# The prologue's 56 stores, moved from SyncE's queue to GpSimd's

## The chip, the cores and the metric

The kernel runs on one core of a Trainium2 chip. Its time is the device time of one execution in microseconds (us), as a median over several runs. The core has five engines that matter here, each working through its own instruction stream in order: TensorE (PE in the profile) multiplies matrices and loads its weights (PEld), VectorE (DVE) and ScalarE (ACT) work element by element, GpSimd (POOL) does likewise but cannot reach the matmul accumulators, and SyncE (SP) computes nothing and only starts transfers. Data move between the chip's main memory and the on-chip memory by DMA transfers. A transfer is started by an instruction in some engine's stream; the data then move by themselves, and a semaphore tells when they have landed.

## The reference, cut to what matters

The reference is one layer of a decoder, run for a prompt of 2048 tokens and for a sample group of 8 sequences with 8 new tokens each, all in float32 with width 1024. The part that the change touches is the memory that the cross-attention reads:

```python
def _mem_kv(mem, g_mem, w_ck, w_cv):
    B = mem.shape[0]
    hm = _rmsnorm(mem, g_mem)
    k = (hm @ w_ck).reshape(B, N_MEM, N_CROSS_HEADS, CROSS_HEAD_DIM)
    v = (hm @ w_cv).reshape(B, N_MEM, N_CROSS_HEADS, CROSS_HEAD_DIM)
    return k, v
...
    x = x + jnp.concatenate([attn_o, pool_o], axis=-1) @ w_out
    h = _rmsnorm(x, g_cross)
    q = (h @ w_cq).reshape(B, L, N_CROSS_HEADS, CROSS_HEAD_DIM)
    s = jnp.einsum('blhd,bmhd->bhlm', q, mem_k).astype(jnp.float32) * (CROSS_HEAD_DIM ** -0.5)
    p = jax.nn.softmax(s, axis=-1)
    o = jnp.einsum('bhlm,bmhd->blhd', p.astype(mem_v.dtype), mem_v).reshape(B, L, D_MODEL)
    x = x + o @ w_co
```

The memory has 256 tokens. Its keys and values `mem_k` and `mem_v` are results of the function as well and must be written out. Beside this the layer has sliding-window attention with 8 heads, a pooling mixer over four windows, and a squared-ReLU MLP of width 4096; these make up most of the work, and the change does not touch them.

## The kernel before

**Number format.** Every product is made of three matmuls (helper `mm3`, lines 110 to 115, and the same pattern in `dense`, lines 317 to 319): each operand is split into a rounded high part and the rest, and high times high, high times low and low times high are added up in one accumulator.

**Weights.** All weights come through one stream (class `Stream`). `emit` (lines 127 to 137) takes one of six staging buffers `f`, starts a load of 512 KB on SyncE's queue (line 133), lets ScalarE round it (line 134) and VectorE take the difference (line 135), and gives the buffer back. Up to five split weights wait ready ahead of TensorE.

**The prologue** (lines 401 to 484) runs first. It has these stages:

1. keys and values of the memory: 16 products with `w_ck` and `w_cv`. `evac` (line 425) multiplies each by the norm on VectorE into a buffer `t` (line 427), stores it to `mk` or `mv` (line 429), and splits it for later use. These are 8 + 8 stores of 128 KB.
2. the fold of `w_cq` with the keys into a matrix A, kept in main memory as `a_s`: 8 weights, two products each, 16 stores of 256 KB.
3. the fold of the values with `w_co` into a matrix B, kept as `b_s`: 4 heads, two weights and four products each, 16 stores of 256 KB.

The fold of the pooling weights with the lower half of `w_out` (function `fold`, line 388) comes a little later, between the first products of the first superblock: four folds with two products each, 8 stores of 256 KB to `wo_s`.

All 40 fold stores go through `put_fold` (line 369): it takes a staging buffer `f` out of the same six that the weight loads use, ScalarE copies the accumulator into it (line 371), a store is started (line 373), and the buffer goes back to the end of the line. Whoever takes that buffer next has to wait until the store has landed. In stage 3 and in `fold` a store goes to four separate places, each row of 128 elements, 512 bytes:

```python
            put_fold(ps[:], lambda o: [(wo_s[4 * eh:4 * eh + 4, :, P * g:P * g + P].rearrange("e p c -> p e c"),
                                        o[:, 0:512].rearrange("p (e c) -> p e c", c=P))])
```

In stage 2 a row of a store is 512 elements, 2 KB, in one piece. The products themselves live in four accumulators `mm`, taken in rotation: a group of matmuls can start when the group four before it has been copied out.

**After the prologue** three superblocks follow, each with the combined input projection (line 879), window attention, the output projection with `woa` and `wo_s`, cross-attention with A and B read back from `a_s` and `b_s`, and the MLP. In them GpSimd scales attention rows (line 746) and adds up the pooling windows (lines 642 to 672).

**Order of the work.** The program order above is the priority, and a planner places the instructions of each engine in the order in which it takes them to become ready. All transfers of the kernel before are started on SyncE's queue, in one order; an instruction there that waits for its data holds up those behind it. The on-chip space for descriptors of transfers begun elsewhere is set where the program is made (line 1390):

```python
    nc = bacc.Bacc("TRN2", target_bir_lowering=False, num_devices=1, dynamic_dma_scratch_size=1024)
```

Of the kernel before, what the change touches and what calls it, by code (L numbers as in the profile page):

```python
# [51 lines left out]
def kernel(ctx: ExitStack, tc: tile.TileContext, io, nW=12, nF=6, nT=8):  # L52
    nc = tc.nc
# [39 lines left out]
    def f32(ap):  # L93
        return ap.bitcast(F32)

    def rnd(ps, hi, lo, scale=None):
        if scale is None:
            nc.scalar.copy(hi, ps)
            nc.vector.tensor_tensor(lo, ps, f32(hi), ALU.subtract)
        else:  # L100
            nc.scalar.activation(hi, ps, AF.Copy, scale=scale)
            nc.vector.scalar_tensor_tensor(lo, ps, scale, f32(hi), ALU.mult, ALU.subtract)
# [4 lines left out]
    def w8(t):  # L107
        return t[:].rearrange("p (k c) -> p k c", c=P)

    def mm3(ps, ks, Wh, Wl, Hh, Hl, first=True, final=True):  # L110
        last = len(ks) - 1
        for i, k in enumerate(ks):
            nc.tensor.matmul(ps, Wh(k), Hh(k), start=first and i == 0, stop=False)  # L113
            nc.tensor.matmul(ps, Wh(k), Hl(k), start=False, stop=False)  # L114
            nc.tensor.matmul(ps, Wl(k), Hh(k), start=False, stop=final and i == last)  # L115
# [226 lines left out]
    def flush(all_=False):  # L342
        for x in list(later):
            x[0] -= 1
            if all_ or x[0] <= 0:
                later.remove(x)
                g = x[1]()
                if g is None:
                    continue
                if all_:  # L350
                    run(g)
                elif next(g, 1) is None:
                    later.append([1, lambda g=g: g])
# [15 lines left out]
    def put_fold(ps, dsts):  # L369
        o = FS.get()  # L370
        nc.scalar.copy(o[:, 0:512], ps)
        for dst, src in dsts(o):
            nc.sync.dma_start(dst, src)
        FS.put(o)

    def prep_fold():
# [11 lines left out]
    def fold(g, wpr):  # L388
        th, tl = S.next(("wop", g))
        for eh in range(2):  # L390
            ps = MM.get()
            mm3(ps[:], [0], lambda k: wpr[:, P * g:P * g + P], lambda k: wpr[:, 512 + P * g:512 + P * g + P],
                lambda k: th[:, 512 * eh:512 * eh + 512], lambda k: tl[:, 512 * eh:512 * eh + 512])
            put_fold(ps[:], lambda o: [(wo_s[4 * eh:4 * eh + 4, :, P * g:P * g + P].rearrange("e p c -> p e c"),
                                        o[:, 0:512].rearrange("p (e c) -> p e c", c=P))])
            MM.put(ps)
        WS.put(th, tl)
        if g == 3:
            WS.put(wpr)

    def prologue():
        S.resW, S.resF = 1, 0
        mx = [XT[1][:, 0:1024], XT[1][:, 1024:2048]]
        mem = lambda k: mx[k // 4][:, 256 * (k % 4):256 * (k % 4 + 1)]
        warm = AUX.get()
        for _ in range(14):
            wu = nc.tensor.matmul(warm[:, 0:P], ones[:], ident[:], start=True, stop=True)
        AUX.put(warm)
        nc.sync.dma_start(vec[:], io["vec"])
        nc.sync.dma_start(mx[0][:, 0:512], io["mem"][:, 0:512])  # L410
        S.emit()
        hm = Act(256)
        nm = Norm(256, mem, add=nc.vector)
        for i in range(4):
            if i:
                nc.sync.dma_start(mx[i // 2][:, 512 * (i % 2):512 * (i % 2) + 512], io["mem"][:, 512 * i:512 * (i + 1)])
            for k in range(2 * i, 2 * i + 2):
                g = vec[:, V_GMEM + k:V_GMEM + k + 1]
                nc.scalar.activation(hm.hi(k), mem(k), AF.Copy, scale=g)
                nc.vector.scalar_tensor_tensor(hm.lo(k), mem(k), g, f32(hm.hi(k)), ALU.mult, ALU.subtract)  # L420
        S.emit()
        for k in range(8):
            nm.sq(k)
        S.pump()
        def evac(a, dst, c, ps):
            t = TS.get()
            nc.vector.tensor_tensor(t[:, 0:256], ps[:, 0:256], nm.r[:, 0:256], ALU.mult)
            MM.put(ps)
            nc.sync.dma_start(dst[:, 256 * c:256 * (c + 1)], t[:, 0:256])
            rnd(t[:, 0:256], a.hi(c), a.lo(c))  # L430
            TS.put(t)

        pend, outs = [], []
        for name, dst in (("ck", io["mk"]), ("cv", io["mv"])):
            a = Act(256)
            outs.append(a)
            for c in range(8):
                th, tl = S.next((name, c))
                ps = MM.get()
                with ExitStack() as held:  # L440
                    if (name, c) == ("ck", 0):
                        held.enter_context(tc.issue_after(wu.ins))
                    mm3(ps[:, 0:256], range(8), lambda k: w8(th)[:, k, :], lambda k: w8(tl)[:, k, :], hm.hi, hm.lo)
                WS.put(th, tl)
                pend.append((a, dst, c, ps))
                if name == "ck" and c == FINC:
                    nm.fin()
                if name == "cv" or c >= FINC:
                    while pend:
                        evac(*pend.pop(0))  # L450
                flush()
                if (name, c) == N1C:
                    norm1(blk[0][0], N1W)
        TS.put(nm.r)
        hm.free()
        mk, mv = outs
        norm1(blk[0][1], N1Q)
        for c in range(8):
            th, tl = S.next(("cq", c))
            for hf in range(2):  # L460
                ps = MM.get()
                for h2 in range(2):
                    ks = [(hf * 2 + h2) * 2, (hf * 2 + h2) * 2 + 1]
                    mm3(ps[:, 256 * h2:256 * h2 + 256], ks, lambda k: w8(th)[:, k, :], lambda k: w8(tl)[:, k, :], mk.hi, mk.lo)
                put_fold(ps[:], lambda o: [(a_s[hf, c // 2, :, 512 * (c % 2):512 * (c % 2) + 512], o[:, 0:512])])
                MM.put(ps)
            WS.put(th, tl)
            flush()
        mk.free()
        for h in range(4):  # L470
            w = [S.next(("co", 2 * h)), S.next(("co", 2 * h + 1))]
            for mb in range(2):
                for eh in range(2):
                    ps = MM.get()
                    mm3(ps[:], range(2),
                        lambda k: mv.hi(2 * h + k, mb * P, mb * P + P), lambda k: mv.lo(2 * h + k, mb * P, mb * P + P),
                        lambda k: w[k][0][:, 512 * eh:512 * eh + 512], lambda k: w[k][1][:, 512 * eh:512 * eh + 512])
                    kt = h * 2 + mb
                    put_fold(ps[:], lambda o: [(b_s[4 * eh:4 * eh + 4, :, P * kt:P * kt + P].rearrange("e p c -> p e c"),
                                                o[:, 0:512].rearrange("p (e c) -> p e c", c=P))])  # L480
                    MM.put(ps)
                flush()
            WS.put(*w[0], *w[1])
        mv.free()
# [17 lines left out]
    def norm1(bl, wait=2):  # L502
        n = bl.n
        if bl.s == 0:
            xs = []
            load_x(bl)
            nm = Norm(n, bl.x)
        else:
            xs = [FS.get() for _ in range(4)]
            for i in range(4):  # L510
                nc.sync.dma_start(xs[i][:, 0:2 * n], io["x"][:, bl.xo + 2 * i * n:bl.xo + 2 * (i + 1) * n])
            nm = Norm(n, lambda k: xs[k // 2][:, n * (k % 2):n * (k % 2) + n])
        for k in range(8):
            nm.sq(k)

        def rest():
            nm.fin()
            bl.h1 = Act(n)
            yield from nm.apply(V_GMIX, bl.h1.hi, bl.h1.lo, PIECE0 if bl.s == 0 else PIECE[0][bl.b])
            FS.put(*xs)  # L520

        later.append([wait, rest])
# [896 lines left out]
```

## Time and profile before

| | before |
|---|---|
| median of 3 runs | 2575.44 us (2572.5 to 2576.32) |
| the profiled execution's own time | 2575.38 us |
| span of its profile | 2573.6 us |
| TensorE busy | 2534.6 us, 98% |
| VectorE, ScalarE, GpSimd busy | 54%, 39%, 7% |
| granted TensorE clock | 0.996 of full |

The span runs from the first to the last instruction of the trace; the execution's own time is 1.8 us longer. "Busy" counts computing instructions only, and matmuls overlap in the pipeline, so that TensorE's 98% is the share of time in which some matmul was under way.

### The profile page before, as it was taken

The numbers are of one execution on the slowest core, as the hardware profiler recorded it, in microseconds if no ns is written. First come the engines' busy times: TensorE is split into PE (matmuls) and PEld (weight loads), VectorE is DVE, ScalarE is ACT, GpSimd is POOL, SyncE is SP. The second block draws the span as 40 slices with busy tenths as digits, with TensorE's granted clock in tenths as the row PEclk, the third lists the DMA queues.
The fourth block names the chain that finished last, engine by engine and source line by source line (L and its number), as shares of the span: only waits on it lengthen the run. The fifth ranks groups of instructions, "written<-read, shape, count | busy, mean of one in ns | idle before, by whom it ended". The sixth has DMA issues, their size and how long they took to land.

```text
span 2573.6 us, 36150 instructions
## 1 busy us (share of the span) xinstructions
PE 2534.6 (98%) x14241; PEld 2315.0 (90%) x14241; DVE 1388.7 (54%) x2797; ACT 998.9 (39%) x2013; POOL 167.4 (7%) x282
## 2 busy tenths in 40 slices
PE   9999999999999999999999999999999999999997
PEld 8798989999999999896788888899989888888886
DVE  8568545444434468774554546887445444434435
ACT  6666343322222234753442324475344322222222
POOL 0015010000000000411000000024010000000000
PEclk9999999999999999999999999999999999999999
DMA  8833212111111125146722222414111111111101
GB/s 284 266 121 102 91 37 78 66 66 66 58 65 66 50 66 160 50 168 213 283 98 93 97 99 75 155 32 148 42 62 54 66 58 58 63 60 58 58 25 54
DMA packets 97614, 245.09 MB, mean 95 GB/s; under 512 B 18916, under 2 KB 37796, under 8 KB 96420
## 3 DMA queue, kind: packets, MB, share of 16 engines
q1 hardware_dynamic: 97444, 242.78, 28.3%
q8 instruction: 112, 1.84, 0.3%
q14 instruction: 58, 0.48, 0.1%
HBM read 219.79 MB, written 22.95 MB: 94 GB/s over the span
## 4 chain that ended last, share of the span: by engine, by line
PE 56%; DVE 2%; ACT 1%; DMA 1%; POOL 0%; issue 0%; DVEq 0%; POOLq 0%; ACTq 0%
PE mm L318 10%; PE mm L317 10%; PE mm L319 10%; PE mm L114 7%; PE mm L113 7%; PE mm L115 7%; PE aux L724 1%; PE aux L755 1%; DVE x L1253 0%; PE aux L968 0%; PE aux L1052 0%; PE aux L114 0%; DVE w L135 0%; PE aux L113 0%; PE aux L115 0%; PE aux L1090 0%
## 5 line engine op out<-in xcount | busy, mean ns | idle before, releaser
L317 PE MATMUL mm<-act,w 128*128 128x384 f32 (+3 forms) x2528 | 857.1, 339 | 2.5 <-ACT act L679 1.6
L319 PE MATMUL mm<-act,w 128*128 128x384 f32 (+3 forms) x2528 | 851.4, 337 | 1.9 <-DVE w L135 1.9
L318 PE MATMUL mm<-act,w 128*128 128x384 f32 (+3 forms) x2400 | 801.8, 334 | 0.7 <-DVE act L680 0.7
L134 ACT CAST w<-f 128x1024 fp32r<-128x1024 f32 x330 | 346.5, 1051 | 818.2 <-PE mm L114 278.3
L113 PE MATMUL mm<-act,w 128*128 128x384 f32 (+3 forms) x1472 | 506.1, 344 | 3.2 <-ACT t L204 2.2
L115 PE MATMUL mm<-act,w 128*128 128x384 f32 (+3 forms) x1472 | 504.8, 343 | 1.9 <-DVE w L135 1.9
L317 PEld LDWEIGHTS mm<-act,w 128*128 128x128 f32 x2528 | 476.7, 189 | 28.3 <-ACT act L679 1.9
L319 PEld LDWEIGHTS mm<-act,w 128*128 128x128 f32 x2528 | 476.4, 188 | 23.1 <-DVE w L135 2.7
L135 DVE TENSOR_TENSOR w<-f,w 128x1024 fp32r<-128x1024 f32 x330 | 402.7, 1225 | 154.7 <-ACT w L134 76.9
L318 PEld LDWEIGHTS mm<-act,w 128*128 128x128 f32 x2400 | 452.6, 189 | 21.1 <-issue 2.5
L114 PE MATMUL mm<-act,w 128*128 128x384 f32 (+3 forms) x1344 | 454.1, 338 | 0.0
L1235 DVE TENSOR_TENSOR x<-mm,x 128x384 f32<-128x384 f32 (+2 forms) x448 | 199.2, 468 | 297.3 <-PE mm L115 297.2
L113 PEld LDWEIGHTS mm<-act,w 128*128 128x128 f32 x1472 | 277.1, 188 | 25.3 <-ACT t L204 2.4
L115 PEld LDWEIGHTS mm<-act,w 128*128 128x128 f32 x1472 | 277.1, 188 | 23.0 <-DVE w L135 2.3
L114 PEld LDWEIGHTS mm<-act,w 128*128 128x128 f32 x1344 | 253.0, 188 | 15.8
L1200 DVE SCALAR_TENSOR_TENSOR t<-mm,t 128x384 f32<-128x384 f32 (+3 forms) x224 | 99.8, 468 | 275.6 <-PE mm L319 275.5
L1201 ACT ACTIVATE t<-t 128x384 f32<-128x384 f32 (+3 forms) x224 | 95.1, 450 | 249.8 <-DVE t L1200 249.8
L1204 DVE TENSOR_TENSOR act<-t,act 128x384 fp32r<-128x384 f32 (+3 forms) x192 | 87.8, 477 | 88.9 <-ACT act L1203 88.9
L113 PE MATMUL mm<-w,act 128*128 128x512 f32 x288 | 114.8, 402 | 1.4 <-ACT w L134 1.3
L114 PE MATMUL mm<-w,act 128*128 128x512 f32 x288 | 113.1, 393 | 1.9 <-DVE w L135 1.8
L115 PE MATMUL mm<-w,act 128*128 128x512 f32 x288 | 112.8, 392 | 0.0
L266 ACT ACTIVATE act<-x,vec 128x384 fp32r<-128x384 f32 (+3 forms) x104 | 57.7, 563 | 106.5 <-DVE x L940 56.4
(210 smaller groups left out, 2200.5 us busy)
## 6 DMA issues: line engine op xcount, KB each, us to landing
f<-in_wup SPq DMA_DIRECT2D x96, 512.0 KB, 3.3
f<-in_wdn SPq DMA_DIRECT2D x96, 512.0 KB, 3.2
f<-in_win SPq DMA_DIRECT2D x30, 512.0 KB, 3.5
f<-a_s SPq DMA_DIRECT2D x24, 512.0 KB, 4.2
f<-b_s SPq DMA_DIRECT2D x24, 512.0 KB, 4.2
x<-in_x SPq DMA_DIRECT2D x6, 1536.0 KB, 8.1
f<-in_wco SPq DMA_DIRECT2D x16, 512.0 KB, 5.3
f<-in_cmk SPq DMA_DIRECT2D x16, 512.0 KB, 4.2
```

What stands on the lines that cost most here:

```text
L113: nc.tensor.matmul(ps, Wh(k), Hh(k), start=first and i == 0, stop=False)
L114: nc.tensor.matmul(ps, Wh(k), Hl(k), start=False, stop=False)
L115: nc.tensor.matmul(ps, Wl(k), Hh(k), start=False, stop=final and i == last)
L134: nc.scalar.copy(th[:], r[:, 0:1024])
L135: eng.tensor_tensor(tl[:], r[:, 0:1024], f32(th[:]), ALU.subtract)
L317: nc.tensor.matmul(ps[:, 0:n], w8(th)[:, k, :], hi(b, k), start=k == 0, stop=False)
L318: nc.tensor.matmul(ps[:, 0:n], w8(th)[:, k, :], lo(b, k), start=False, stop=False)
L319: nc.tensor.matmul(ps[:, 0:n], w8(tl)[:, k, :], hi(b, k), start=False, stop=k == 7)
L1200: nc.vector.scalar_tensor_tensor(r[:, 0:n], ps[:, o:o + n], 0.0, p.bl.r3[:, p.c0:p.c0 + n], ALU.max, ALU.mult)
L1201: nc.scalar.activation(q[:, 0:n], r[:, 0:n], AF.Square)
L1204: nc.vector.tensor_tensor(lo, q[:, 0:n], f32(hi), ALU.subtract)
L1235: nc.vector.tensor_tensor(p.x(m), ps[:, p.o:p.o + p.n], p.x(m), ALU.add)
```

## The change

Two lines start their transfers from GpSimd's queue (`nc.gpsimd`) instead of SyncE's (`nc.sync`). The first is in `put_fold`, which makes the 40 stores of fold products, the second in `evac`, which makes the 16 stores of memory keys and values. Sources, destinations, sizes and buffers stay as they are, and all loads stay on SyncE's queue.

```diff
@@ -370,7 +370,7 @@
         o = FS.get()
         nc.scalar.copy(o[:, 0:512], ps)
         for dst, src in dsts(o):
-            nc.sync.dma_start(dst, src)
+            nc.gpsimd.dma_start(dst, src)
         FS.put(o)
@@ -426,7 +426,7 @@
             t = TS.get()
             nc.vector.tensor_tensor(t[:, 0:256], ps[:, 0:256], nm.r[:, 0:256], ALU.mult)
             MM.put(ps)
-            nc.sync.dma_start(dst[:, 256 * c:256 * (c + 1)], t[:, 0:256])
+            nc.gpsimd.dma_start(dst[:, 256 * c:256 * (c + 1)], t[:, 0:256])
             rnd(t[:, 0:256], a.hi(c), a.lo(c))
             TS.put(t)
```

## The prediction

> **What bounds the kernel now.** I read the page's first lines, then the busy time by stretches of the prologue, then what TensorE waits for there, then the transfers.
>
> ```profile
> span 2573.6 us, 36150 instructions
> PE 2534.6 (98%) x14241; PEld 2315.0 (90%) x14241; DVE 1388.7 (54%) x2797; ACT 998.9 (39%) x2013; POOL 167.4 (7%) x282
> ...
> core 0: us, PE busy (x) PEld busy (x) DVE busy (x) ACT busy (x) POOL busy (x), PEclk, DMA share, GB/s
> 63.00:90.00 27.00, 25.53 (x190) 23.86 (x190) 22.34 (x36) 20.27 (x39) 0.46 (x1) 1.00 0.81 253
> 90.00:118.00 28.00, 25.44 (x110) 19.34 (x109) 10.09 (x11) 16.33 (x25) 0.00 (x0) 1.00 0.96 287
> 118.00:145.00 27.00, 24.00 (x118) 21.16 (x117) 15.15 (x22) 16.59 (x28) 0.00 (x0) 0.94 0.76 233
> ```
>
> TensorE sets the time, with 2534.6 of 2573.6 us. The change acts between 24 and 145 us. The three stretches are the A fold, the B fold, and the first input products with the pooling folds; in them TensorE lacks 1.5 + 2.6 + 3.0 = 7.1 us. That is the most a better order of transfers there can give. In the B stretch the DMA engines are at 96%: there the transfers themselves fill the time.
>
> ```profile
> PE mm L113 <- ACT t L204: 2.2, 1, 2.2
> PE mm L113 <- ACT w L383: 2.0, 1, 2.0
> PE mm L115 <- DVE w L135: 1.9, 2, 1.2
> PE mm L114 <- DVE w L135: 1.8, 3, 0.8
> ```
>
> Of TensorE's waits up to 165 us (total, times, longest) the first is a norm and has no transfer in it; the other three are for weights that came late.
>
> ```profile
> SPq L373 <- ACT f L371: 28.6, 25, 4.6
> SPq L429 <- DVE t L427: 28.2, 15, 6.2
> ```
>
> These are SyncE's own waits at the moved lines: 57 us in which the store at the head of the queue waited for ScalarE's or VectorE's copy, with loads queued behind it. That is what the change takes away.
>
> **The change part by part.** It moves 56 instructions that start transfers: 16 in `evac`, 40 in `put_fold`. No store becomes smaller, and no load moves.
>
> ```profile
> L373 SPq DMA_DIRECT2D a_s<-f x16: 319/326/1625, 65.0 to 87.7; - x16
> L373 SPq DMA_DIRECT2D b_s<-f x16: 359/498/1901, 90.5 to 116.3; - x16
> L373 SPq DMA_DIRECT2D wo_s<-f x8: 359/377/422, 125.9 to 141.4; - x8
> ```
>
> (Shortest, median and longest start in ns, first and last start.) On SyncE they take some 0.33 to 0.50 us each, about 20 us for the 40; SyncE is no bound, so this saving is worth nothing by itself. On POOL there is room:
>
> ```profile
> 54.61 0.25 POOL L612 COPY x<-ucar 128x15 f32<-128x15 f32 x1 [53.31 <-DVE t L258]
> ...
> 69.68 0.46 POOL L612 COPY x<-ucar 128x15 f32<-128x15 f32 x1 [7.49 <-DVE t L258]
> 163.36 1.11 POOL L746 TENSOR_SCALAR x<-x,st 128x128 f32<-128x128 f32 x3 [93.22 <-DVE st L742]
> ```
>
> POOL computes nothing in the prologue except four copies that are wanted only later; the first work that TensorE will wait for is L746 at 163.4 us. What a start costs on POOL, the trace does not show. Bounds: 0.32 us (the shortest start on SP) and 2.2 us (the shortest landing of these stores, below). The B stage brings 16 stores in 28 us, one per 1.75 us, so any price up to 1.75 us is hidden. I take about 1 us, nearest to the 4.16 us that four waiting starts took on SP (next fence), and count nothing for it.
>
> Removed waits: without the stores ahead of them the loads may start earlier. The bounds are a gain of 7.1 us, were all the lacking TensorE time to go, and nothing, since loads also wait for one of the six `f` buffers, and these wait for landings:
>
> ```profile
> 90.47 4.16 SPq L373 DMA_DIRECT2D b_s<-f  x4
> ...
> 69.12 1.21 ACT L371 COPY f<-mm 128x512 f32<-128x512 f32 x2 [2.08 <-DMA a_s<-f]
> ...
> 104.96 1.20 ACT L371 COPY f<-mm 128x512 f32<-128x512 f32 x2 [0.20 <-DMA b_s<-f]
> ```
>
> ScalarE already waits here for an `f` buffer whose store has not landed. So the term that decides is how long a store holds its buffer.
>
> ```profile
> q1 hardware_dynamic: 8894, 7.99, 95.2%
> ...
> b_s<-f SPq DMA_DIRECT2D x16, 256.0 KB, 5.6
> ...
> a_s<-f SPq DMA_DIRECT2D x16, 256.0 KB, 4.4
> ...
> wo_s<-f SPq DMA_DIRECT2D x8, 256.0 KB, 3.0
> ...
> out_mk<-t SPq DMA_DIRECT2D x8, 128.0 KB, 2.4
> ...
> DMA to landing us min/median/max: 2.2/4.8/6.2
> ```
>
> (The first two lines are of 90 to 118 us: packets, MB, share; then KB each and median us to landing.) In that stretch 16 stores and 7 loads make 8894 packets: a store of 256 KB in rows of 512 bytes is 512 packets, 8192 together, and the loads have the rest, some 100 each. The stores of `wo_s` have the same form, those of `a_s`, `mk` and `mv` are 128 rows each.
>
> On SP up to four such stores are under way at a time, one for each `f` buffer that is not with a load (in the B stage four stores and two loads share the six). On POOL the trace shows no transfer, so I bound from both sides: they overlap as on SP, or a store of 512 packets starts only when the one before it has landed. I take the second for `b_s` and `wo_s`, and overlap for the others: the code reserves 1024 bytes (line 1390) for describing such transfers, and 512 packets are much to describe in that, 128 four times less. [...]
>
> The price of one at a time: let T be the time from a store's start to the next one's. The 24 stores (16 B, 8 pooling) then land at 90.5 + kT. With four buffers, the copy of store 22 needs store 18 landed, and the first input product behind the last fold needs that copy, by the rotation of four `mm`. Before, that product started here:
>
> ```profile
> 140.54 0.33 PE L317 MATMUL mm<-act,w 128*128 128x384 f32 x1
> ```
>
> With 0.6 us for the copy (two took 1.21 us above), TensorE is late by 90.5 + 18T + 0.6 - 140.5 = 18T - 49.4 us. T lies between 3.0 us (`wo_s`, same form and size) and 5.6 us (`b_s` at 95% DMA load, with loads ahead of it in its own queue). One at a time the engines are less full, so I start from 3.0 us and add the start of about 1 us, which nothing overlaps: T = 4.0 us, and 18 x 4.0 - 49.4 = 22.6 us. The ends are 4.6 us (T = 3.0) and 51.4 us (T = 5.6). Nothing later gives it back, as TensorE is busy 98% of the span.
>
> What is late next:
>
> ```profile
> 149.97 0.43 SPq L133 DMA_DIRECT2D f<-wo_s  x1
> 167.44 0.33 SPq L133 DMA_DIRECT2D f<-in_woa  x1
> ```
>
> The first read of `wo_s` needs all folds landed: 90.5 + 24 x 4.0 = 186.5 us, against 150.0 + 22.6 = 172.6. SyncE stands 14 us there, but the next load behind it is not wanted before 167.4 + 22.6 = 190 us, so this is hidden up to T = 4.1 us, and beyond that five ready weights cover it. On POOL the last store starts at 90.5 + 23 x 4.0 = 182.5 us, ahead of L746 at 163.4 + 22.6 = 186: hidden, by 2.5 us net of the start.
>
> Sum: the profiled execution's 2575.38 us (0.06 below the median of the runs shown) + 22.6 = 2598.0 us.
>
> **The rivals.** *The stores overlap on POOL as on SP* and SyncE's loads start earlier: between 2575.4 - 7.1 = 2568.3 and 2575.4 us. The 57 us of waits speak for it. Against a large gain speak the 96% DMA share of the B stage, which leaves at most the 1.5 and 3.0 us of its neighbours, 2.0 of which hang on L383's one late load. I'd expect 2572. It decides as soon as two 512-packet stores can be under way. This is the rival on the other side.
>
> *One at a time, but quick.* Below T = 49.4 / 18 = 2.74 us TensorE is not held, and the time stays at 2575.4. The shortest landing of 2.2 us and `mk`'s 2.4 us speak for it; both `b_s` and `wo_s` medians lie above. [...]
>
> *A start on POOL costs over 1.75 us.* At the upper bound of 2.2 us the B stage takes 16 x 2.2 - 28 = 7.2 us more: 2582.6 us. The longest start on SP, 1.9 us, would cost 2.4 us.
>
> *All 40 fold stores go one at a time.* Then store 34 of the 40, counted from the first `a_s` at 65.0 us, is the one waited for: 65.0 + 34T + 0.6 - 140.5 = 34T - 74.9; with T = 3.0, for 128 rows are lighter, 27.1 us: 2602.5. The smaller packet count of `a_s` speaks against it.
>
> **How the numbers follow.** One at a time with T above 3.03 us: 0.57. Overlap: 0.20, half of it a gain of over 0.2%, half none. Quick: 0.10. POOL's start: 0.07. All 40: 0.06. About 0.2%, 5.2 us, is what a measurement of this kernel can tell from no change. Slower is 0.57 + 0.07 + 0.06 = 0.70, the same 0.10 + 0.10 = 0.20, faster 0.10. The range reaches from 2571, which takes in most of the overlap case, to 2627, T = 5.6; the forecast's own range is 2580 to 2627.
>
> **What would show it.** In the changed profile: L373 on POOL's queue; `b_s` starts 3 to 5.6 us apart instead of 1.75, each after the landing before it; `a_s` starts as close as before; ScalarE's L371 waiting for `b_s` landings by many us; the B stretch of TensorE stretched, its idle time there some 20 us; the rest of the trace shifted and otherwise the same. I am wrong if two `b_s` stores are under way at once, if the time lost lies after 190 us, or if the A stretch grows as much as the B stretch.

## The result

The changed kernel is **slower**, by 1.3%: 2608.41 us, median of 4 runs (2607.21 to 2612.48), against 2575.88 us for the kernel before beside it (4 runs, 2572.5 to 2576.88). The difference of the medians is 32.5 us; the ratio on record, which is not worked out from the two medians alone (they give 1.0126), is 1.0132, with a 95% interval of 1.012 to 1.0144. One of the ten executions of act_queue below took 3113 us and is left out of its figures; with it its median is 2578.74 us. The forecast was 2598.0 us, or 22.6 us slower, with a range of 2571 to 2627. The side and the mechanism were right, the size was 10 us short, and the forecast came that near partly by luck (see the part on the prediction).

The profiled execution took 2612.48 us, 4.1 us more than its kernel's median. Numbers read from the trace below are therefore a little larger than the 32.5 us that the medians show.

The first lines of the page after, and its DMA queues (packets, MB, share):

```profile
span 2610.7 us, 36174 instructions
...
PE 2546.5 (98%) x14241; PEld 2326.2 (89%) x14241; DVE 1388.3 (53%) x2797; ACT 999.5 (38%) x2013; POOL 202.1 (8%) x338
...
q1 hardware_dynamic: 80164, 230.19, 25.5%
q0 software_dynamic: 3968, 12.59, 1.4%
```

The move happened: POOL has 56 more instructions, and a queue of the software kind carries the 12.59 MB. TensorE's matmuls are the same in number; the span grew by 37.1 us, its busy time by 11.9 us, so two thirds of the loss is idle time of TensorE.

Busy time by stretches, after (columns as in the prediction; the last row is a new stretch):

```profile
63.00:90.00 27.00, 25.17 (x188) 24.41 (x187) 21.37 (x34) 18.72 (x35) 8.48 (x17) 0.94 0.73 239
90.00:118.00 28.00, 20.36 (x79) 13.75 (x77) 10.40 (x14) 13.97 (x22) 6.42 (x9) 1.00 0.59 203
118.00:145.00 27.00, 16.03 (x70) 13.27 (x69) 5.44 (x9) 8.60 (x16) 6.06 (x8) 0.87 0.38 122
145.00:165.00 20.00, 9.02 (x35) 8.27 (x35) 7.33 (x10) 7.34 (x12) 3.78 (x5) 0.66 0.52 163
```

The A fold, 63 to 90 us, is nearly as before (25.17 us busy against 25.53). Behind it TensorE lacks 28.00 - 20.36 = 7.6 us, then 11.0 and 11.0 us. The DMA share, 0.96 in the B stretch before, is 0.59: the transfers no longer fill the time, they wait to be started. In the last two rows the granted clock has fallen as well, to 0.87 and 0.66.

The moved instructions themselves (shortest, median, longest in ns, first and last start; then what POOL's idle time before them ended with, and who waited for them):

```profile
L373 POOL DMA_DIRECT2D a_s<-f x16: 542/542/552, 66.7 to 93.2; - x16
L373 POOL DMA_DIRECT2D b_s<-f x16: 752/761/784, 95.3 to 145.2; - x16
L373 POOL DMA_DIRECT2D wo_s<-f x8: 752/757/762, 150.3 to 179.9; - x8
...
  issue: 59.3, 21
...
  ACT f L371: 36.9, 16
```

The 16 `b_s` stores, which started within 25.8 us before, now take 49.9 us, or 49.87 / 15 = 3.32 us apart; the 8 of `wo_s` are 29.6 / 7 = 4.23 us apart. A start itself is short, 0.54 us with 128 rows and 0.76 us with 512. Yet POOL sat idle for 59.3 us in front of 21 of them for "issue", that is for nothing that the profile shows. POOL's timeline (start, duration, idle time before and its releaser):

```profile
66.74 2.42 POOL L373 DMA_DIRECT2D a_s<-f  x4 [3.08 <-ACT f L371]
...
95.33 0.78 POOL L373 DMA_DIRECT2D b_s<-f  x1 [1.62 <-ACT f L371]
...
110.03 0.76 POOL L373 DMA_DIRECT2D b_s<-f  x1 [2.32 <-issue]
113.05 0.75 POOL L373 DMA_DIRECT2D b_s<-f  x1 [2.26 <-issue]
...
179.90 0.75 POOL L373 DMA_DIRECT2D wo_s<-f  x1 [3.12 <-DVE w L135]
```

Four `a_s` stores go in 2.42 us without a pause, while GpSimd pauses for 2.3 us and more in front of each `b_s` store: 0.75 + 2.26 = 3.01 us is the shortest spacing. Before, four `b_s` stores on SyncE started within 4.16 us. What the pauses end with can be seen beside ScalarE's copies that wait for a `b_s` landing:

```profile
109.83 0.59 ACT L371 COPY f<-mm 128x512 f32<-128x512 f32 x1 [2.48 <-DMA b_s<-f]
```

The next two such copies start at 112.85 and 115.86 us. Each time a store starts 0.2 us later (110.03, 113.05, 116.07), before that copy is finished, so it is the store of an earlier copy: GpSimd and ScalarE waited for the same landing.

Where TensorE feels it (its waits up to 250 us: total, times, longest):

```profile
PE mm L113 <- ACT f L371: 12.5, 8, 3.0
PE mm L113 <- DVE w L540: 10.8, 1, 10.8
PE mm L113 <- ACT w L383: 5.5, 1, 5.5
```

The first row is what was forecast: copies (L371) that wait for a buffer whose store has not landed. The other two weren't: waits for the split of the pooling weights (L383, 2.0 us before), and for an accumulator from which ScalarE (L539) and VectorE (L540) still read the projected attention keys (`put_k`). How a store comes to hold up these can be followed from SyncE's waits between 90 and 185 us, through its next start, to ScalarE's and TensorE's timelines:

```profile
SPq L133 <- DMA b_s<-f: 16.5, 2, 12.2
```

```profile
145.37 0.33 SPq L133 DMA_DIRECT2D f<-in_win  x1
```

```profile
141.97 0.59 ACT L371 COPY f<-mm 128x512 f32<-128x512 f32 x1 [1.93 <-DMA b_s<-f]
149.35 1.04 ACT L134 CAST w<-f 128x1024 fp32r<-128x1024 f32 x1 [6.80 <-DMA f<-in_win]
...
153.72 1.04 ACT L134 CAST w<-f 128x1024 fp32r<-128x1024 f32 x1 [2.83 <-DMA f<-in_wop]
154.67 0.47 ACT L539 CAST w<-mm 64x384 fp32r<-64x384 f32 x1
```

```profile
126.97 0.44 PE L317 MATMUL mm<-act,w 128*128 128x384 f32 x1 [1.64 <-ACT f L371]
...
144.35 0.40 PE L114 MATMUL mm<-w,w 128*128 128x512 f32 x1
144.59 0.40 PE L115 MATMUL mm<-w,w 128*128 128x512 f32 x1
155.79 0.79 PE L113 MATMUL mm<-w,w 128*128 128x512 f32 x1 [10.81 <-DVE w L540]
156.38 0.63 PE L114 MATMUL mm<-w,w 128*128 128x512 f32 x1
156.81 0.63 PE L115 MATMUL mm<-w,w 128*128 128x512 f32 x1
157.24 0.52 PE L317 MATMUL mm<-act,w 128*128 128x384 f32 x1
...
171.25 0.44 PE L317 MATMUL mm<-act,w 128*128 128x384 f32 x1
```

A `w_in` load needs a buffer `f` that a `b_s` store still holds. SyncE waits 12.2 us for that store, and starts the load at 145.37. ScalarE takes its instructions in order, and the cast of that load (L134) stands ahead of the cast L539, whose matmuls had ended by 145.0 us: it waits 6.80 us, and the cast of the next load, which SyncE starts at 150.04 after waiting another 4.3 us for a `b_s` store, 2.83 us more. Only then comes L539, VectorE's L540 behind it, and the accumulator is free; TensorE has stood for 10.81 us. The buffers and ScalarE's order tie these loads and casts to the stores, though the change didn't touch them.

The three lines L317 in the fence are the starts of the first input product, of the third, and of the fifth, which stands behind the last fold. The first two of these stood before at

```profile
112.27 0.44 PE L317 MATMUL mm<-act,w 128*128 128x384 f32 x1 [0.31 <-ACT f L371]
...
128.40 0.44 PE L317 MATMUL mm<-act,w 128*128 128x384 f32 x1 [0.32 <-ACT w L134]
```

and the third at 140.54. So TensorE is late by 14.7, 28.8 and 30.7 us: nearly half is lost by the end of the B fold, the other half between the first and third input product, and little behind. The other half is the two unforeseen waits: 5.5 - 2.0 + 10.8 = 14.3 us.

### The profile page after: what moved, and what is told of

It reads as the page before. It is cut to its first block, busy times and chain, and to the rows that moved or that the text cites. A ratio compares the mean times of both kernels' runs of the same rounds, so it can differ in the third digit from the quotient of the medians.

```text
span 2610.7 us, 36174 instructions
## 1 busy us (share of the span) xinstructions
PE 2546.5 (98%) x14241; PEld 2326.2 (89%) x14241; DVE 1388.3 (53%) x2797; ACT 999.5 (38%) x2013; POOL 202.1 (8%) x338
## 3 DMA queue, kind: packets, MB, share of 16 engines
q0 software_dynamic: 3968, 12.59, 1.4%
## 4 chain that ended last, share of the span: by engine, by line
PE 55%; DVE 1%; POOL 1%; ACT 1%; DMA 0%; issue 0%; DVEq 0%; ACTq 0%; POOLq 0%
PE mm L318 10%; PE mm L319 10%; PE mm L317 10%; PE mm L113 7%; PE mm L114 7%; PE mm L115 7%; PE aux L724 1%; PE aux L755 1%; POOL t L642 0%; PE aux L1052 0%; DVE x L1253 0%; PE aux L968 0%; PE aux L113 0%; PE aux L115 0%; PE aux L114 0%
## 5 line engine op out<-in xcount | busy, mean ns | idle before, releaser
L317 PE MATMUL mm<-act,w 128*128 128x384 f32 (+3 forms) x2528 | 859.3, 340 | 3.6 <-ACT f L371 1.6
L134 ACT CAST w<-f 128x1024 fp32r<-128x1024 f32 x330 | 346.3, 1051 | 817.4 <-PE mm L114 274.1
L317 PEld LDWEIGHTS mm<-act,w 128*128 128x128 f32 x2528 | 478.5, 189 | 29.5 <-ACT f L371 2.1
L319 PEld LDWEIGHTS mm<-act,w 128*128 128x128 f32 x2528 | 478.5, 189 | 22.7 <-DVE w L135 2.2
L114 PEld LDWEIGHTS mm<-act,w 128*128 128x128 f32 x1344 | 254.4, 189 | 15.6
```

The costliest lines, as they stand in the source:

```text
L134: nc.scalar.copy(th[:], r[:, 0:1024])
L317: nc.tensor.matmul(ps[:, 0:n], w8(th)[:, k, :], hi(b, k), start=k == 0, stop=False)
L319: nc.tensor.matmul(ps[:, 0:n], w8(tl)[:, k, :], hi(b, k), start=False, stop=k == 7)
```

## The experiments

The theory, called 'room' in what was expected of the runs: on POOL's queue a store of 512 rows has to wait until the one before it is done, because the 1024 bytes of line 1390 hold the description of one such store (its entries, as split4's expectation has it) and not of two. Its rivals: POOL's start as such is slow; the 512-byte rows are slow to write from there; the loss comes from something else that was moved, such as the wide stores. Behind that stands a second question: why the loss is 32.5 us and not 22.6.

All medians, with the ratio to the kernel before that was measured beside each:

| run | what differs | median us | ratio (95%) |
|---|---|---|---|
| after | all 56 stores on POOL, 1024 bytes | 2608.41 | 1.0132 (1.012 to 1.0144) |
| ring1088 | 1088 bytes | 2585.89 | 1.0032 (1.0018 to 1.0045) |
| ring1728 | 1728 bytes | 2579.94 | 1.0016 (1.0005 to 1.0026) |
| only_wide | only the stores of 128 rows on POOL | 2575.61 | 0.9994 (0.9985 to 1.0003) |
| only_512 | only the stores of 512 rows on POOL | 2610.26 | 1.0128 (1.0113 to 1.0143) |
| split4 | each 512-row store cut into four | 2589.6 | 1.0058 (1.0042 to 1.0075) |
| act_queue | fold stores on ScalarE's queue | 2577.2 | 1.0009 (0.9995 to 1.0023) |
| apart_after | after, buffers of stores and loads apart | 2602.79 | 1.011 (1.0093 to 1.0127) |
| apart_before | before, buffers apart | 2572.22 | 0.999 (0.9981 to 1.0) |
| early_after | after, pooling weights early | 2613.59 | 1.0141 (1.0127 to 1.0155) |
| early_apart_after | after, both edits | 2604.04 | 1.0111 (1.0096 to 1.0127) |
| early_apart_before | before, both edits | 2571.78 | 0.9987 (0.9978 to 0.9997) |
| early_apart_1728 | after, both edits, 1728 bytes | 2580.64 | 1.0015 (1.0006 to 1.0024) |

### More room for descriptors

```diff
-dynamic_dma_scratch_size=1024
+dynamic_dma_scratch_size=1088
```

and the same with 1728.

> All 56 stores from GpSimd as in the changed kernel; only the space kept for their descriptors (line 1390) grows from 1024 to 1088 bytes. [...] Then two b_s stores are under way at once, their starts come 1.7 to 2.5 us apart instead of 3.3, and most of the 32.5 us goes: 2575 to 2588 us. Rival 'landing': GpSimd begins no such store before the last has landed, whatever the space: starts 3.3 us apart and 2605 to 2612 us.

> As the changed kernel, with 1728 bytes for the descriptors: three stores of 512 rows fit by the theory 'room'. It expects 2572 to 2580 us, b_s starts set by the copies again (1.75 us apart), and no more idle time before them on GpSimd than before any other store. Rival 'landing': 2605 to 2612 us, as at 1024 bytes. If it lies above 2580 while the b_s stores overlap, something else of the move costs, such as the later landings of mk and mv.

Sixty-four bytes more take about 23 us of the 32.5 us away: 2585.89 us, 9.6 us above the kernel before beside it. POOL's timeline with 1088 bytes shows how:

```profile
107.60 1.50 POOL L373 DMA_DIRECT2D b_s<-f  x2 [3.10 <-issue]
111.32 1.50 POOL L373 DMA_DIRECT2D b_s<-f  x2 [2.22 <-issue]
115.31 1.60 POOL L373 DMA_DIRECT2D b_s<-f  x2 [2.49 <-issue]
```

The pauses are as long as before, but now two stores go behind each: a pair every 3.7 to 4.0 us. With 1728 bytes (the moved instructions' group):

```profile
L373 POOL DMA_DIRECT2D b_s<-f x16: 752/752/770, 92.6 to 119.0; - x16
...
  issue: 9.0, 7
```

the 16 stores start within 26.4 us, much as on SyncE (25.8), POOL's pauses shrink from 59.3 to 9.0 us, and 3.6 us of the loss are left. Nothing but the reserved space was changed in either, so the space sets how many such stores can be under way, and with it most of the loss.

That two such stores have room in 1088 bytes and only one in 1024 was the author's estimate; the runs agree: the pairs appear at 1088. If two take twice the space of one, these two runs put it at over 512 and at most 544 bytes for a store of 512 rows, so that 1728 bytes hold three and not four; this is an estimate from the two runs, and what the space is filled with they do not show. That GpSimd waits when its space is used up is read from its idle time for "issue" in front of the stores: 59.3 us before 21 of them with 1024 bytes, 17.1 us before 9 with 1088, 9.0 us before 7 with 1728.

### Wide stores alone, 512-row stores alone

```diff
-    def put_fold(ps, dsts):
+    def put_fold(ps, dsts, eng=nc.gpsimd):
...
-            nc.gpsimd.dma_start(dst, src)
+            eng.dma_start(dst, src)
```

with `eng=nc.sync` for `b_s` and `wo_s` in one kernel, and for `a_s` (and line 429 on SyncE) in the other.

> Only the stores of 128 rows (mk, mv and a_s, 32 of them) begin on GpSimd's queue; the 24 stores of 512 rows (b_s, wo_s) stay on SyncE's. [...] Rival 'every GpSimd start costs': 32 of 56 moved, so more than half of the loss stays, 2592 us or more.

> Only the 24 stores of 512 rows (b_s, wo_s) begin on GpSimd's queue; mk, mv and a_s stay on SyncE's. Theory 'room': the whole serial part stays: 2600 to 2610 us, b_s starts 3.0 to 3.5 us apart. Rival 'every GpSimd start costs': 24 of 56, so less than half of the loss: 2590 us or less.

The 32 wide stores alone cost nothing that can be measured (2575.61 us, interval across 1; 'room' expected 2573 to 2581), although the A stage ends 2.8 us late by 84 us; that is regained by 128 us. The 24 narrow ones alone cost all of it, 33.9 us. POOL's timeline of the latter:

```profile
140.80 0.76 POOL L373 DMA_DIRECT2D b_s<-f  x1 [2.26 <-issue]
143.81 0.76 POOL L373 DMA_DIRECT2D b_s<-f  x1 [2.25 <-issue]
```

The same pause stands there with no other store on the queue. Only_wide also shows what SyncE's waits were worth: with the wide stores moved, the 28.2 us at L429 have left its queue, with a part of those at L373, and the time is the same.

### Narrow rows or many descriptors

The same bytes in the same 512-byte rows, as four stores of 128 rows each, 1024 bytes reserved:

```diff
-                    put_fold(ps[:], lambda o: [(b_s[4 * eh:4 * eh + 4, :, P * kt:P * kt + P].rearrange("e p c -> p e c"),
-                                                o[:, 0:512].rearrange("p (e c) -> p e c", c=P))])
+                    put_fold(ps[:], lambda o: [(b_s[4 * eh + e, :, P * kt:P * kt + P], o[:, P * e:P * e + P]) for e in range(4)])
```

and likewise for `wo_s`: 96 transfers instead of 24.

> As the changed kernel with 1024 bytes, but each store of 512 rows is four stores of 128 rows of the same 512 bytes (96 transfers for 24). [...] Rival 'short rows': it is the 512-byte rows and not the number of entries that make GpSimd go one at a time: 2605 us or more.

2589.6 us, where 'room' expected 2580 to 2595: 18.8 us are regained though there are four times as many starts. POOL's timeline:

```profile
115.43 18.06 POOL L373 DMA_DIRECT2D b_s<-f  x33 [0.85 <-DMA b_s<-f]
```

33 starts in 18.06 us, 0.55 us each, without a pause among them. Rows of 512 bytes are thus not the trouble, nor is the reserved space by itself: it is the size of a single transfer's description against that space. What is left of the loss here is 13.8 us. POOL is now busy with starting: four times 0.55 us is 2.2 us per group, above the 1.75 us that the B stage has for one. By the working of the prediction's third rival that is 16 x 2.2 - 28 = 7.2 us; the other half was not taken apart.

### Another queue

Fold stores begun by ScalarE behind its own copy; keys and values on SyncE:

```diff
-            nc.sync.dma_start(dst, src)
+            nc.scalar.dma_start(dst, src)
```

> The 40 fold stores begin on ScalarE's queue, right behind the copy that feeds them; mk and mv stay on SyncE's. Theory 'room': ScalarE's queue showed no such limit on SyncE's kind of transfer, so the stores overlap, no load waits behind a store, and the cost is ScalarE's time for 40 starts, 0.3 to 0.5 us each, partly beside its idle time: 2570 to 2582 us. Rival 'leaving SyncE's queue is what costs': 2590 us or more.

2577.2 us, no difference that can be told. No kernel run before this one had started a transfer from ScalarE, so this is the first to show that its queue has no such limit here, with the same 1024 bytes in line 1390. The `b_s` stores start within 25.4 us there:

```profile
L373 ACTq DMA_DIRECT2D b_s<-f x16: 366/438/1377, 96.1 to 121.5; - x16
```

The first of them starts at 96.1 us, as late as in the kernel after (95.3), and nothing comes of it. So leaving SyncE's queue is harmless by itself, and worth nothing, the 28.6 us of SyncE's waits at L373 included: the loss belongs to POOL's queue with its reserved space.

### Why 32.5 and not 22.6: the shared buffers and the pooling weights

Two edits each take one of the unforeseen waits away. In the first, between the first and the last fold store, four of the six `f` buffers serve stores and two only loads. (One of the four goes to a tile that the first superblock keeps, `v32`; for the pooling folds three are left.)

```diff
+    def fget(store):
+        if apart[0] is None:
+            apart[0] = {id(t) for t in list(FS.free)[0:4]}
+        t = next(t for t in FS.free if (id(t) in apart[0]) == store)
+        FS.free.remove(t)
+        return t
...
-        o = FS.get()
+        o = fget(True)
```

In the second, the pooling weights are loaded and split before the B fold, into other buffers:

```diff
-        wpr = WS.get()
+        wpr = ACTS.get()
...
-        wp = FS.get()
+        wp = TS2[0]
...
         mk.free()
+        wprs.append(prep_fold())
```

The first, and both together, were also run on the kernel before, to see what they are worth without the change; the second alone was not.

> As the changed kernel, but from the first fold store to the last four of the six f buffers serve stores (and the long-lived v32) only, and two serve loads only, so that no weight load inherits a buffer from a store. Theory 'late weights': of the 32.5 us some 10 come from the loads of win, wop and wpool that waited for a b_s store's landing; TensorE's waits for L540 and L383 (16.3 us) fall below 6, and what stays is the stores' own chain: 2590 to 2600 us. Rival 'the stores' rate alone': the end is set by when the last folds are stored, however the loads come: 2605 to 2612 us.

> The same rule for the f buffers with all stores on SyncE's queue, as a control for the run beside it. Both theories expect little: 2571 to 2580 us, since landings on SyncE's queue hold no load for long.

> As the changed kernel, with the pooling weights loaded and split before the B fold (into buffers outside the six f buffers) instead of behind it. TensorE's wait for L383, 5.5 us in the changed kernel, goes, and wpool no longer takes a turn among the f buffers. Theory 'stalls add up': TensorE has too little work behind such a stall to make it good while the stores run, so the time falls by that stall, 5 us or more: 2598 to 2604 us. Rival 'the stores' chain alone': the end is set by when the 22nd store has a buffer, and the wait only moves to another line: 2606 to 2611 us.

> Both: pooling weights early, and f buffers of stores and loads kept apart, with all stores from GpSimd and 1024 bytes. Theory 'stalls add up': from the 2602.8 us with the buffers apart another 7 us (the wait for the pooling weights there) go: 2593 to 2598 us, and what is left is copies waiting for landings. Rival 'the stores' chain alone': 2600 to 2605 us, as with the buffers apart only.

> The same two edits with all stores on SyncE's queue: a version that may beat both kernels. From 2572.2 us with the buffers apart, the wait for the pooling weights of 1.7 us goes too: 2566 to 2572 us if later stages do not give it back; 2572 to 2576 if they do, as the attention behind it gave back some 3 of the 5 us won by 150 us in the run with buffers apart alone.

Buffers apart give 2602.79 us, less than was hoped for (2590 to 2600). SyncE's wait for `b_s` landings is gone (16.5 us to none), but TensorE's waits up to 250 us have changed places (L380, L392 and L550 are L371, L383 and L540 of the kernel after):

```profile
PE mm L113 <- ACT f L380: 13.8, 10, 2.4
PE mm L113 <- ACT w L392: 7.1, 1, 7.1
PE mm L113 <- DVE w L550: 5.6, 1, 5.6
```

The wait at L540 is halved, the other two have grown. ScalarE's timeline tells why the pooling weights are late although their load has its own buffer now and started at 124.10 us:

```profile
136.27 0.58 ACT L380 COPY f<-mm 128x512 f32<-128x512 f32 x1 [3.99 <-DMA b_s<-f]
136.75 1.27 ACT L392 ACTIVATE w<-f,vec 128x128 fp32r<-128x128 f32 x4
```

The split stands behind a copy in ScalarE's order, and the copy waits for a landing. With the pooling weights early the wait at L383 is gone, and the time is 2613.59 us, no better than after and above both expected ranges:

```profile
PE mm L113 <- ACT f L371: 16.1, 12, 2.5
PE mm L113 <- DVE w L540: 11.5, 1, 11.5
```

The waits for copies have grown by 3.6 us and the one at L540 by 0.7 us, most of its 5.5 us. Both edits together give 2604.04 us, as the first alone. On the kernel before they give 2572.22 and 2571.78 us; the pair's interval, 0.9978 to 0.9997, lies just under 1. That is the lowest median of all kernels run here, 4.6 us under the kernel before beside it, a gain of less than 0.2% and with no store on POOL; the 0.4 us between it and the first edit alone cannot be told from nothing.

So the single stalls do not add up: take one away and the time goes into the next. What stays the same is the row of 24 stores. Its last start, in the one profiled execution of each and measured from the 141.4 us of the kernel before, and the loss of the medians:

| run | last `wo_s` start later by, us | loss, us |
|---|---|---|
| after | 38.5 | 32.5 |
| only_512 | 43.0 | 33.9 |
| early_after | 44.5 | 37.3 |
| early_apart_after | 39.3 | 27.7 |
| apart_after | 32.6 | 26.9 |
| split4 | 15.6 | 13.8 |
| ring1088 | 11.8 | 9.6 |
| early_apart_1728 | 6.3 | 4.7 |
| act_queue | 5.7 | 1.4 |
| ring1728 | 3.3 | 3.6 |
| only_wide | 0.0 | -0.7 |
| early_apart_before | -3.7 | -4.6 |
| apart_before | -4.1 | -3.6 |

The two go together over the whole range. That is a correlation and not a proof: a late last store and a late TensorE can also follow each other in a circle, since a store waits for a product and a product for a buffer. That the row of stores leads is argued from POOL's pauses without a releaser, 59.3 us in front of 21 starts in the kernel after, and from the starts 0.2 us behind a landing.

### What is left with enough room

With 1728 bytes and both edits, the question was whether the last 3.6 us belong to the pooling weights' wait that ring1728 shows (L383, 4.9 us) or to the queue.

> All 56 stores from GpSimd, 1728 bytes for the descriptors, pooling weights early, f buffers of stores and loads kept apart. Theory 'room': with three stores under way the move itself costs nothing that can be measured, and the two edits win what they win on SyncE's queue: 2568 to 2575 us. Rival 'a rest of the cost belongs to the queue', the 3.6 us above before that 1728 bytes left: 2575 to 2580 us.

2580.64 us, just above both expected ranges: that wait is gone, the loss is still 4.7 us (interval 1.0006 to 1.0024), and against the same two edits on the kernel before it is 2580.64 - 2571.78 = 8.9 us, though the two were not measured beside each other. So a rest belongs to the queue even where, by the estimate above, three stores have room. The `b_s` stores of these two kernels, from SyncE's queue and from GpSimd's, say where it arises:

```profile
L382 SPq DMA_DIRECT2D b_s<-f x16: 359/378/1017, 87.7 to 111.9; - x16
...
L382 POOL DMA_DIRECT2D b_s<-f x16: 750/750/767, 97.7 to 124.4; - x16
```

The first of them is 10.0 us late, and the last `wo_s` store (147.7 against 137.7 us) is 10.0 us late as well. So here the rest is there before the first store of 512 rows, in the A stage: at 60 us TensorE is level with the kernel before, and between 60 and 102 us it waits 6.1 us for copies (L380), and not once for one in the other kernel. What makes the A stage late was not taken apart. In the kernels with the wide stores on POOL TensorE is 1.1 us (apart_after) to 5.3 us (early_apart_1728) behind the kernel before by 84 us, and the landings of `mk` are longer (median 6.1 to 6.4 us in after, ring1088, ring1728 and only_wide, against 2.4 before); but act_queue is 3.4 us behind there with no store on POOL, and it and only_wide lost nothing that can be measured. For ring1728, 1.9 us behind by 84 us, it is not settled whether its rest is the wait at L383: the edits that took this wait away also moved its first `b_s` start from 92.6 to 97.7 us.

## Why the prediction was right in kind and short in size

**What bounds the kernel, the removed waits, the saving on SyncE.** Right. Of the 57 us of SyncE's waits, only_wide takes the half at L429 away and act_queue the half at L373; they are at 0.9994 and 1.0009.

**The start on POOL.** About 1 us was taken, bounds 0.32 and 2.2; it is 0.54 us for 128 rows and 0.76 us for 512. Hidden, as said; the third rival falls for this kernel, and split4 shows it where it does hold.

**One store at a time.** Right, and shown by ring1088: 64 bytes decide. How many bytes one such store takes was the author's estimate and is in no trace; by the estimate from the runs above it is between 512 and 544. Overlap, the first rival, comes to pass when two or three stores fit. "Quick" needed T under 2.74 us; the shortest spacing is 3.01. "All 40" falls by the four `a_s` starts in 2.42 us.

**T.** Taken as 4.0 us, built of a landing of 3.0 and a start of 1.0 that nothing overlaps. Measured: 3.32 us for `b_s`, 4.23 for `wo_s`, over all 24 stores (179.90 - 95.33) / 23 = 3.68. The landings after (KB each, median us) are

```profile
b_s<-f POOLq DMA_DIRECT2D x16, 256.0 KB, 2.8
...
wo_s<-f POOLq DMA_DIRECT2D x8, 256.0 KB, 4.1
```

They are counted from the start, and the spacing is only some 0.1 to 0.5 us more. So the start lies within the landing and the 1.0 us was not to be added; that `wo_s` would land in 4.1 us instead of 3.0 was not foreseen. T was too large; alone it would have made the forecast too high, not too low. There lies the luck: 18 x 0.32 = 5.8 us too many in T made up for part of what the next step left out.

**The step that failed** is "the copy of store 22 needs store 18 landed, and the first input product behind the last fold needs that copy", with the sum 18T - 49.4 made from it. With what was measured, store 18 starts at 154.7 us (the second `wo_s` start) and lands some 3.0 us later; with 0.6 us for the copy the product would be late by 154.7 + 3.0 + 0.6 - 140.5 = 17.8 us. It was late by 30.7. The step counted one way from the stores to TensorE, the four `mm` and the buffers of the copies. There are two more: loads take the same buffers (the `w_in` load, 12.2 us of SyncE's wait, 10.8 us of TensorE's), and ScalarE's order puts casts behind copies that wait (L383, 5.5 us). Instead of 18 stores in the sum, the whole row of 24 tells the size better, though that was seen afterwards and rests on the correlation above: from first to last start it took 50.9 us before (90.47 to 141.4) and takes 84.6 us now, 33.6 us more, against 32.5 us lost. In terms of the prediction that is 23T - 50.9, with T = 3.68.

**The A stage.** Counted at nothing; it made the first `b_s` start 4.9 us late (95.3 instead of 90.5), of which the formula knew nothing. In only_wide and act_queue such a delay cost nothing that can be measured, in early_apart_1728 it seems to be the whole rest, so it is open how much of it is in the 32.5 us.

**What is late next.** Right: the first read of `wo_s` starts at 185.3 us (forecast 186.5), and POOL's L746 comes at 195.1 instead of 163.4 us, shifted by 31.7 like the rest; neither adds to the loss.

**Signs.** The `b_s` spacing, ScalarE's waits for landings and the stretched B stage came as said. The `a_s` starts came close together, though not quite as close as before (16 within 26.5 us instead of 22.7). "Idle time there some 20 us" did not: 7.6 us lie in the B stretch and 22 us in the two behind it. "The rest only shifted" holds for the most part: late by 30.7 us behind the last fold, by 33.4 us at 300 us and by 36.9 us from about 1650 us on. The last 3.5 us are about what this one execution lies above its median; where they come from is open.

## What to carry to other kernels

Before a transfer is moved to GpSimd's queue, count its rows against the space reserved for descriptors, and ask how many such transfers are to be under way at once: one too few cost a full landing per transfer here (2.8 us for `b_s`, 4.1 us for `wo_s`), and 64 bytes decided it. A queue's own waits are worth only what TensorE waits for them; either half of the 57 us was worth nothing here. When a store becomes slower, follow its buffer to all who take it next, loads included, and look at what stands behind each waiting instruction in an in-order engine: the stall that one edit removes goes into the next, and the length of the whole chain is the better measure.

## What the hardware showed beside this

**A wait that names no cause.** GpSimd's wait for room appears as idle time with the releaser "issue", in after and only_512 most often of 2.25 to 2.28 us. Whoever looks for a semaphore finds none; a run with more reserved space names it, and so do copies on another engine that go at the same moments.

**Clock.** The 10.8 us of idle time cost more than themselves. Between 150 and 156 us (columns as above):

```profile
150.00:156.00 6.00, 0.21 (x1) 0.21 (x2) 2.58 (x4) 3.13 (x6) 1.51 (x2) 0.50 0.41 131
```

the granted clock was 0.50, and of the matmuls of 512 columns behind the pause the second and third started 0.43 us apart (156.38 and 156.81), where the last two before it started 0.24 us apart (144.35 and 144.59). The granted clock was 0.50 behind the pause of 5.5 us at L383 too (134 to 140 us), and still 1.00 behind one of 2.4 us (119 to 122 us). At which length of pause between these two the clock falls is not shown.

**Landing of small stores.** The transfers on POOL's queue (KB each, median us to landing):

```profile
out_mk<-t POOLq DMA_DIRECT2D x8, 128.0 KB, 6.4
```

It was 2.4 us on SyncE's queue. It cost nothing measurable in only_wide.

**Packets.** The page counts 3968 packets for the 12.59 MB on POOL's queue, some 3.2 KB each, where the rows of 24 of the 56 stores are 512 bytes. Those 24 stores alone have 24 x 512 = 12288 such rows. On this queue the packet count is no measure of the rows to be described, and so did not show the limit that decided.

**GpSimd and the accumulators.** In the traces before and after no instruction on GpSimd reads or writes an accumulator (`mm`, `aux`); whether it could, no run tried.
